# Weight low parts made by accumulating DMAs from GpSimd's queue, and softmax normalization moved from GpSimd to VectorE

## The chip, the cores and the metric

The kernel runs on one core of a Trainium2 chip. The metric is the device time of one execution in microseconds. The kernel before takes 1223.67 us, the median of three runs (1223.36 to 1224.05).

## The reference

One sequence of 512 tokens of width 1024 goes through two transformer blocks, all in float32.

- First block: RMS norm, one wide projection `h @ w_in`, then two attention branches of 8 heads each. One branch keeps the 128 best keys of each query by an indexer score (`relu(q_idx . k_idx)` weighted and summed over 8 index heads); the other is "forgetting" attention, with a cumulative log gate added to its logits. Each branch is gated by a silu and projected; two sigmoid gates from `h @ w_merge` merge the branches; `w_out`, a norm and a gated per-layer embedding (`w_ple`, `w_ple_gate`) follow.
- Second block: RMS norm, a projection `w_in_2`, sliding-window attention with sinks (8 heads), latent attention (8 heads, with `w_uq_2` and `w_ukv_2`), gates `ga` and `gb`, `w_out_2`, then a feed-forward layer `(silu(h @ w_gate_2) * (h @ w_up_2)) @ w_down_2` of inner width 2816, and a final norm.

The weights are float32 and each is read once from HBM. What the document is about is how a weight becomes two matmul operands:

```
w  =  hi + lo          hi = w rounded to the matmul type,  lo = w - hi
x @ w  ~  xh @ hi + xh @ lo + xl @ hi
```

## The kernel before

Every product with a weight runs as three TensorE matmuls (line 345): high by high, activation high by weight low, activation low by weight high. Activations are split into `hh` and `hl` (or `h2h`, `x2h`, `acts`, `fs` and so on) by `split`.

Weights come in one stream of tiles, in an order fixed when the program is built (`stream`, `first_of`). A tile is 128 partitions by at most 1024 columns, 512 KB, mostly two 128-row slices of a 512-column product. For each tile:

- `load_to` issues a DMA on SP's queue into a buffer `raw`, of which there are two;
- `convert_to` rounds it on ScalarE into `wh` (line 260) and subtracts on VectorE to get `wl = raw - wh` (line 261). There are four buffers `wh` and four `wl`. Where `fine[0]` is set, in the interleaved attention stages, both are done in two halves;
- `product` reads both. After the last matmul that reads tile i, `used` calls `convert_to(i + 4)`, which takes the buffers that tile i has left.

The feed-forward's gate and up weights after the first 512 columns go another way (`Quarters`, seven products of quarters, `quart` and `qsum`); they use the same lines 260 and 261. The tile "misc" is made of five column ranges.

`product` has an order. With "mid" it goes through the weight tiles one after the other, four token blocks on each, so that a tile is done with every 24 matmuls. With "all" it goes through all four tiles for the first block, then for the second and so on: the four buffers stay taken until the last block, are released about six matmuls apart, and the next product wants its first tile as soon as this one ends. The name of a product is used in the following for the place where it begins: "the boundary into gb1" is where gb1 follows gb0.

The attention stages are recorded by `interleave`: a step of attention (scores, softmax, and two or three steps later the transposes of the probabilities, then the product with the values) alternates with matmuls of products. There, and in pg1 with q2 and in o21 with fg0 and the quarters, TensorE's order is that of the code (`ordered`). Elsewhere a scheduler orders the instructions of all engines. Each engine and each DMA queue takes its instructions in order.

In `softmax_step`, VectorE adds the mask (line 522), ScalarE exponentiates and sums (line 529), VectorE takes the reciprocal `rr` (line 535), and GpSimd multiplies the probabilities `P` by it (line 537, since `NORM = "pool"`). GpSimd also computes the exponent's bias in the forgetting branch (line 527) and every norm's variance and `rstd` (lines 452 to 463). Before the change it issues no DMA.

Of the kernel before, what the change touches and what calls it, by code (L numbers as in the profile page):

```python
# [13 lines left out]
AF = mybir.ActivationFunctionType  # L14
OP = mybir.AluOpType
# [13 lines left out]
def two_blocks_kernel(  # L29
# [7 lines left out]
    nc = tc.nc  # L37
    pool = ctx.enter_context(tc.tile_pool(name="sb", bufs=1))
# [29 lines left out]
    def blk(i):  # L68
        return slice(i * 128, (i + 1) * 128)

    NORM = "pool"
    TOPK_EVERY = 3
    FOX_EVERY = 3
    IDX = (1.5, 2, 2, 0.5)
# [156 lines left out]
    raws, ws = [], []  # L231
# [3 lines left out]
    def load_to(i):  # L235
        while len(raws) <= min(i, len(stream) - 1):
            pieces, k0, nk, ncols = stream[len(raws)]
            if isinstance(pieces, Quarters):
                raws.append(pieces.load_for(k0))
                continue  # L240
            raw = pool.tile([128, 1024], F32, name="raw", tag="raw", bufs=2)
            raw = raw[:, :nk * ncols].rearrange("p (k c) -> p k c", c=ncols)
            for w, c0, n, at in pieces:
                nc.sync.dma_start(
                    raw[:, :, at:at + n],
                    w[k0 * 128:(k0 + nk) * 128, c0:c0 + n].rearrange("(k p) c -> p k c", p=128))
            raws.append(raw)

    def convert_to(i):
        while len(ws) <= min(i, len(stream) - 1):  # L250
            load_to(len(ws))
            pieces, k0, nk, ncols = stream[len(ws)]
            raw = raws[len(ws)]
            if isinstance(raw, Quarters):
                raw = raw.part(k0)
            hi, lo = [pool.tile([128, 1024], FR, name=t, tag=t, bufs=4)[:, :nk * ncols].rearrange(
                "p (k c) -> p k c", c=ncols) for t in ("wh", "wl")]
            cut = (nk + 1) // 2 if fine[0] else nk
            for js in [slice(j, min(nk, j + cut)) for j in range(0, nk, cut)]:
                nc.scalar.copy(hi[:, js], raw[:, js])  # L260
                mark[0] = nc.vector.tensor_sub(lo[:, js], raw[:, js], hi[:, js].bitcast(F32)).ins  # L261
            ws.append((hi, lo))

    def used(i):
        spent.add(i)
        while upto[0] in spent:
            upto[0] += 1
        convert_to(upto[0] + 3)
        last = min(upto[0] + 5, len(stream) - 1)
        load_to(last - isinstance(stream[last][0], Quarters))  # L270

    side = []
    mark = [None]
# [15 lines left out]
    def product(name, act, evac, tok, order="mid", parts=4, ready=None):  # L289
# [35 lines left out]
        for i, (t, n0, nn, kc) in enumerate(seq):  # L325
            while ready and not ready(kc):
                yield 0
            if t not in ps:
                spare = t == 3 and (ready or order != "all" or ordered_[0] and not fine[0])
                ps[t] = s_bank("mm") if spare else mm_bank()  # L330
            g, j = divmod(kc, step)
            convert_to(f0 + g)
            wh, wl = ws[f0 + g]
            ah, al = act(kc)
# [183 lines left out]
    def softmax_step(Sb, n, mask, sink=None, cq=None):  # L518
# [16 lines left out]
        nc.vector.reciprocal(rr, rs)  # L535
        if NORM == "pool":
            nc.gpsimd.tensor_scalar(P[:, :n], P[:, :n], rr, 1.0, op0=OP.mult, op1=OP.mult)  # L537
# [120 lines left out]
    for tb in range(NB):  # L658
        for c in halves if tb == 0 else [slice(0, 1024)]:
            nc.sync.dma_start(xs[:, tb, c], xv[:, tb, c])  # L660
        if tb == 0:
            gb = g_bcast(g_pre)
        convert_to(tb)
        fine[0] = False
# [144 lines left out]
    def qk_shared(qs, kt, h, Sb, qb, k0, n):  # L809
        nc.tensor.matmul(Sb[:, :n], qs[:, h, blk(qb)], kt[:, 0, k0:k0 + n], start=True, stop=False)  # L810
        nc.tensor.matmul(Sb[:, :n], qs[:, h, blk(qb)], kt[:, 1, k0:k0 + n], start=False, stop=True)  # L811
# [21 lines left out]
    for qb in range(1, NB):  # L833
        n = (qb + 1) * 128
# [59 lines left out]
    for pi in range(4):  # L894
        pair = Pair(lambda att, pi=pi: half_gated(att, aa, pi))
        for h in (2 * pi, 2 * pi + 1):
            steps += causal_head(
                h, lambda Sb, qb, k0, n, h=h: qk_shared(qa, kik[1], h, Sb, qb, k0, n), lambda kb: va[:, kb, :], pair,
# [570 lines left out]
```

## Time and profile before

| What | Value |
|---|---|
| median of three runs | 1223.67 us |
| the profiled execution's own time | 1223.95 us |
| its span, first to last instruction | 1222.2 us |
| TensorE busy | 1188.5 us, 97% of the span |
| VectorE busy | 821.8 us, 67% |
| ScalarE busy | 615.0 us, 50% |
| GpSimd busy | 157.5 us, 13% |
| mean granted TensorE clock | 0.997 |

The shares of the other engines are averages over stages with different loads. TensorE's 97% is the one that matters here: 33.7 us of the span are not matmul. What other engines do costs time only where TensorE has to wait for it. The timeline view has start and duration in microseconds, then the engine, the line, the operation, output and inputs; a release in brackets says how long the engine was idle before and what ended that.

### The profile page before, as it was taken

The numbers are of one execution on the slowest core, as the hardware profiler recorded it, in microseconds if no ns is written. First come the engines' busy times: TensorE is split into PE (matmuls) and PEld (weight loads), VectorE is DVE, ScalarE is ACT, GpSimd is POOL, SyncE is SP. The second block draws the span as 40 slices with busy tenths as digits, with TensorE's granted clock in tenths as the row PEclk, the third lists the DMA queues.
The fourth block names the chain that finished last, engine by engine and source line by source line (L and its number), as shares of the span: only waits on it lengthen the run. The fifth ranks groups of instructions, "written<-read, shape, count | busy, mean of one in ns | idle before, by whom it ended". The sixth has DMA issues, their size and how long they took to land.

```text
span 1222.2 us, 18908 instructions
## 1 busy us (share of the span) xinstructions
PE 1188.5 (97%) x6876; PEld 1030.8 (84%) x6876; DVE 821.8 (67%) x1792; ACT 615.0 (50%) x1290; POOL 157.5 (13%) x307
## 2 busy tenths in 40 slices
PE   6999999999999999999999999999999999999997
PEld 5898888888888888689888889778899999988885
DVE  5578767896676554775555688773887878783322
ACT  4465456545563343534566567632555555472212
POOL 2011033101120022601211112200000000000201
PEclk9999999999999999999999999999999999999999
DMA  5422302321232532324232211353333332253221
GB/s 191 99 68 69 121 19 70 93 87 35 69 105 86 189 121 87 118 86 108 69 89 67 63 62 54 98 172 110 121 104 95 114 107 92 62 173 120 87 86 69
DMA packets 78780, 117.19 MB, mean 96 GB/s; under 512 B 10336, under 2 KB 41312, under 8 KB 78688
## 3 DMA queue, kind: packets, MB, share of 16 engines
q1 hardware_dynamic: 78688, 115.99, 30.1%
q8 instruction: 54, 0.88, 0.3%
q14 instruction: 38, 0.31, 0.1%
HBM read 109.68 MB, written 6.29 MB: 95 GB/s over the span
## 4 chain that ended last, share of the span: by engine, by line
PE 84%; DVE 6%; issue 3%; POOL 2%; ACT 2%; DMA 2%; SPq 0%; POOLq 0%; ACTq 0%; DVEq 0%
PE mm L345 57%; PE mm L1311 7%; PE R L1311 5%; PE E L1311 5%; PE AV L592 3%; PE T L577 3%; DVE wl L261 1%; PE S L810 1%; PE S L811 1%; PE T L476 1%; ACT wh L260 1%; DMA raw<-in_w_in_dram 1%; PE T L1103 1%; DMA quart<-in_w_up_dram 1%; POOL var L461 1%
## 5 line engine op out<-in xcount | busy, mean ns | idle before, releaser
L261 DVE TENSOR_TENSOR wl<-raw,wh 128x512 fp32r<-128x512 f32 (+6 forms) x203 | 186.1, 936 | 139.6 <-ACT wh L260 138.5
L260 ACT CAST wh<-raw 128x512 fp32r<-128x512 f32 (+6 forms) x203 | 158.1, 804 | 192.3 <-PE mm L345 127.8
L345 PE MATMUL mm<-wh,fs 128*128 128x512 f32 x352 | 110.6, 395 | 1.6 <-ACT fs L447 1.6
L537 POOL TENSOR_SCALAR P<-P,rr 128x256 f32<-128x256 f32 (+3 forms) x128 | 68.7, 537 | 310.4 <-DVE rr L535 218.9
L345 PE MATMUL mm<-hh,wh 128*128 128x512 f32 x256 | 103.6, 405 | 0.0
L345 PE MATMUL mm<-hl,wh 128*128 128x512 f32 x256 | 101.4, 396 | 0.0
L345 PE MATMUL mm<-hh,wl 128*128 128x512 f32 x256 | 100.3, 395 | 0.0
L445 DVE TENSOR_TENSOR pl<-T,ph 128x128 fp32r<-128x128 f32 (+3 forms) x152 | 62.3, 412 | 28.7 <-ACT ph L444 28.1
L345 PEld LDWEIGHTS mm<-wh,fs 128*128 128x128 f32 x352 | 65.9, 188 | 18.1 <-ACT fs L447 1.8
L444 ACT CAST ph<-T 128x128 fp32r<-128x128 f32 (+3 forms) x152 | 54.9, 362 | 49.4 <-PE T L577 36.6
L529 ACT ACTIVATE P<-P,nm 128x128 f32<-128x128 f32 (+2 forms) x96 | 51.5, 536 | 47.1 <-DVE nm L522 41.5
L260 ACT CAST wh<-qsum 128x1024 fp32r<-128x1024 f32 (+1 forms) x44 | 42.7, 974 | 54.6 <-PE R L1311 23.2
L345 PE MATMUL mm<-wl,fs 128*128 128x512 f32 x176 | 69.7, 397 | 0.3 <-DVE wl L261 0.3
L261 DVE TENSOR_TENSOR wl<-qsum,wh 128x1024 fp32r<-128x1024 f32 (+1 forms) x44 | 49.5, 1126 | 13.4 <-ACT wh L260 13.4
L1311 PE MATMUL R<-acts,wh 128*128 128x256 f32 x320 | 57.8, 281 | 0.0
L1311 PE MATMUL mm<-acts,wh 128*128 128x256 f32 x320 | 57.6, 280 | 0.0
L345 PEld LDWEIGHTS mm<-hh,wl 128*128 128x128 f32 x256 | 48.0, 188 | 11.2
L1311 PE MATMUL E<-acts,wh 128*128 128x256 f32 x320 | 57.1, 280 | 0.0
L577 PE MATMUL T<-ident,P 128*128 128x128 f32 x296 | 54.5, 277 | 2.4 <-DVE km L445 1.2
L345 PEld LDWEIGHTS mm<-hh,wh 128*128 128x128 f32 x256 | 48.2, 188 | 8.5
L345 PEld LDWEIGHTS mm<-hl,wh 128*128 128x128 f32 x256 | 48.2, 188 | 7.8
L345 PE MATMUL mm<-h2h,wh 128*128 128x512 f32 x128 | 53.4, 417 | 0.0
(392 smaller groups left out, 3344.3 us busy)
## 6 DMA issues: line engine op xcount, KB each, us to landing
raw<-in_w_in_dram SPq DMA_DIRECT2D x50, 512.0 KB, 3.6
raw<-in_w_down_dram SPq DMA_DIRECT2D x22, 512.0 KB, 3.7
quart<-in_w_up_dram SPq DMA_DIRECT2D x20, 512.0 KB, 4.0
raw<-in_w_merge_dram SPq DMA_DIRECT2D x16, 512.0 KB, 3.5
raw<-in_w_out_dram SPq DMA_DIRECT2D x16, 512.0 KB, 3.7
quart<-in_w_gate_dram SPq DMA_DIRECT2D x16, 512.0 KB, 3.7
raw<-in_w_ple_gate_dram SPq DMA_DIRECT2D x8, 512.0 KB, 3.8
raw<-in_w_branch_b_dram SPq DMA_DIRECT2D x4, 512.0 KB, 3.5
```

What stands on the lines that cost most here:

```text
L260: nc.scalar.copy(hi[:, js], raw[:, js])
L261: mark[0] = nc.vector.tensor_sub(lo[:, js], raw[:, js], hi[:, js].bitcast(F32)).ins
L345: nc.tensor.matmul(o, x_, m, start=kc == 0 and k == 0 and n0 == 0, stop=last and k == 2)
L444: nc.scalar.copy(hi, src)
L445: nc.vector.tensor_sub(lo, src, hi.bitcast(F32))
L461: nc.gpsimd.tensor_scalar(v, ss[:, 1:2], 1.0 / n, v, op0=OP.mult, op1=OP.add)
L476: nc.tensor.transpose(T[:, i, :], src[:, blk(c + i)], ident)
L529: nc.scalar.activation(P[:, :n], P[:, :n], AF.Exp, bias=bias, scale=-1.0, accum_out=rs)
L537: nc.gpsimd.tensor_scalar(P[:, :n], P[:, :n], rr, 1.0, op0=OP.mult, op1=OP.mult)
L577: nc.tensor.transpose(T[:, i, :], P[:, blk(i)], ident)
L592: nc.tensor.matmul(self.av[:, q0:q0 + pc.stop - pc.start], self.v(kb), m, start=pi == 0 and i == 0, stop=pi == len(plan) - 1 and i == 1)
L1311: nc.tensor.matmul(R[:, c, :], w[:, kc, cs], m[:, kc, :], start=first and c + kc + k == 0, stop=kc == 3 and k == 2, skip_group_check=True)
```

## The change

For a weight tile of one column range (not "misc", not the quarters, and not the first four tiles of the program), the low part is no longer subtracted on VectorE. ScalarE writes the rounded tile negated into `wl`; then a DMA issued from GpSimd's queue reads the weight a second time from HBM and adds it to what stands in `wl`. The two halves of the `fine` stages fall away for these tiles: there is one instruction of each kind per tile. And the probabilities are multiplied by the reciprocal on VectorE.

```
-    NORM = "pool"
+    NORM = "dve"
...
             hi, lo = [pool.tile([128, 1024], FR, name=t, tag=t, bufs=4)[:, :nk * ncols].rearrange(
                 "p (k c) -> p k c", c=ncols) for t in ("wh", "wl")]
+            if len(ws) > 3 and not isinstance(pieces, Quarters) and len(pieces) == 1:
+                w, c0, n, _ = pieces[0]
+                nc.scalar.copy(hi, raw)
+                mark[0] = nc.scalar.activation(lo, raw, AF.Copy, scale=-1.0).ins
+                nc.gpsimd.dma_start(lo, w[k0 * 128:(k0 + nk) * 128, c0:c0 + n].rearrange("(k p) c -> p k c", p=128),
+                                    accum_op=OP.add)
+                ws.append((hi, lo))
+                continue
             cut = (nk + 1) // 2 if fine[0] else nk
```

Lines after the added ones are eight higher in the changed kernel: line 345 is 353 there, 537 to 539 are 545 to 547.

ScalarE's queue at the boundary into gb1, before (`wh` and `raw` are the weight tile, `tb` a gate's output, `ph` the high part of transposed probabilities, `P` the probabilities, `es` the sink's term):

```order
L444 CAST ph<-T 128x128
L260 CAST wh<-raw 128x512 x2
L444 CAST ph<-T 128x128
L260 CAST wh<-raw 128x512 x2
L529 ACTIVATE P,rs<-P,nm 128x256
L532 ACTIVATE es<-sk,nm 128x1
L444 CAST ph<-T 128x128 x2
L529 ACTIVATE P,rs<-P,nm 128x256
L532 ACTIVATE es<-sk,nm 128x1
L864 ACTIVATE tb_5905<-mm 128x512
L260 CAST wh<-raw 128x512 x4
L529 ACTIVATE P,rs<-P,nm 128x128
```

ScalarE's queue at the same place, with the change:

```order
L872 ACTIVATE tb_5940<-mm 128x512
L452 CAST ph<-T 128x128
L260 CAST wh<-raw 128x1024
L261 ACTIVATE wl<-raw 128x1024
L452 CAST ph<-T 128x128
L260 CAST wh<-raw 128x1024
L537 ACTIVATE P,rs<-P,nm 128x256
L540 ACTIVATE es<-sk,nm 128x1
L261 ACTIVATE wl<-raw 128x1024
L452 CAST ph<-T 128x128
L260 CAST wh<-raw 128x1024
L261 ACTIVATE wl<-raw 128x1024
```

What VectorE did in halves now stands on ScalarE behind the rounding, as one instruction, in front of the exponentials and splits of the attention steps.

GpSimd's queue in the forgetting attention, before (`bias` is the exponent's bias, `P` the probabilities):

```order
L527 TENSOR_SCALAR bias<-nm,ctok 128x1
L537 TENSOR_SCALAR P<-P,rr 128x128
L527 TENSOR_SCALAR bias<-nm,ctok 128x1
L537 TENSOR_SCALAR P<-P,rr 128x256
L527 TENSOR_SCALAR bias<-nm,ctok 128x1
L537 TENSOR_SCALAR P<-P,rr 128x384
```

GpSimd's queue there with the change (`in_w_merge_dram` are the weights of ma0 and ma1, which run inside this stage):

```order
L262 DMA wl<-in_w_merge_dram 128x2x512 x3
L535 TENSOR_SCALAR bias<-nm,ctok 128x1
L262 DMA wl<-in_w_merge_dram 128x2x512
L535 TENSOR_SCALAR bias<-nm,ctok 128x1 x13
L262 DMA wl<-in_w_merge_dram 128x2x512
L535 TENSOR_SCALAR bias<-nm,ctok 128x1
L262 DMA wl<-in_w_merge_dram 128x2x512 x2
```

The multiplications have left GpSimd, and the weights' DMAs stand between the biases. Each DMA waits at the head of this queue until ScalarE has written its tile.

VectorE's queue in the same stage with the change (`S` are the scores, `pl` the low part of the transposed probabilities):

```order
L543 RECIPROCAL rr<-rs 128x1
L530 ISA P,nm<-S,causal 128x256
L530 ISA nm 128x1
L547 TENSOR_SCALAR P<-P,rr 128x128
L543 RECIPROCAL rr<-rs 128x1
L530 ISA P,nm<-S,causal 128x384
```

The multiplication is queued one mask step behind its reciprocal.

## Rows read from the trace of the kernel before

**Rows 1.** The page: busy time of each engine, share of span, instructions.

```profile
PE 1188.5 (97%) x6876; PEld 1030.8 (84%) x6876; DVE 821.8 (67%) x1792; ACT 615.0 (50%) x1290; POOL 157.5 (13%) x307
```

**Rows 2.** What TensorE waited for: us in total, times, longest.

```profile
PE T L476 <- DVE xn L670: 9.6, 1, 9.6
PE T L476 <- DVE xn L484: 4.0, 3, 2.2
PE mm L345 <- DVE wl L261: 3.0, 3, 2.2
...
PE T L577 <- POOL P L537: 0.2, 1, 0.2
```

**Rows 3.** Groups by form: busy us, mean ns, then idle time before.

```profile
L261 DVE TENSOR_TENSOR wl<-raw,wh 128x1024 fp32r<-128x1024 f32 x88 | 110.5, 1259 | 116.8 <-ACT wh L260 116.5
L260 ACT CAST wh<-raw 128x1024 fp32r<-128x1024 f32 x88 | 92.3, 1049 | 150.3 <-PE mm L345 112.5 <-issue 19.4 <-DMA raw<-in_w_in_dram 5.4
L537 POOL TENSOR_SCALAR P<-P,rr 128x256 f32<-128x256 f32 x48 | 25.1, 524 | 104.7 <-DVE rr L535 54.2 <-ACT ph L444 12.9 <-ACT ta L864 10.6
L527 POOL TENSOR_SCALAR bias<-nm,ctok 128x1 f32<-128x1 f32 x32 | 11.7, 365 | 43.9 <-DVE nm L522 43.5
```

**Rows 4.** Timeline at the boundary into gb1: its third weight tile.

```profile
658.92 1.77 SPq L244 DMA_DIRECT2D raw<-in_w_in_dram  x2
...
662.69 1.13 ACT L260 CAST wh<-raw 128x512 fp32r<-128x512 f32 x2
...
664.28 0.69 DVE L261 TENSOR_TENSOR wl<-raw,wh 128x512 fp32r<-128x512 f32 x1
...
665.02 0.39 PE L345 MATMUL mm<-h2h,wl 128*128 128x512 f32 x1
```

**Rows 5.** Timeline, tight boundaries: subtraction and first reader, into vb and dn0.

```profile
100.41 1.71 DVE L261 TENSOR_TENSOR wl<-raw,wh 128x512 fp32r<-128x512 f32 x2
...
102.05 0.39 PE L345 MATMUL mm<-wl,hh 128*128 128x512 f32 x1
...
1087.35 1.22 DVE L261 TENSOR_TENSOR wl<-raw,wh 128x1024 fp32r<-128x1024 f32 x1
...
1088.62 0.74 PE L345 MATMUL mm<-wl,fs 128*128 128x512 f32 x2 [0.33 <-DVE wl L261]
```

**Rows 6.** Timeline, middle boundaries: the same pair, into mb0 and o21.

```profile
280.56 1.22 DVE L261 TENSOR_TENSOR wl<-raw,wh 128x1024 fp32r<-128x1024 f32 x1
...
283.94 0.39 PE L345 MATMUL mm<-hh,wl 128*128 128x512 f32 x1
...
837.87 1.23 DVE L261 TENSOR_TENSOR wl<-raw,wh 128x1024 fp32r<-128x1024 f32 x1 [0.43 <-ACT wh L260]
...
840.98 0.39 PE L345 MATMUL mm<-wl,yh 128*128 128x512 f32 x1
```

**Rows 7.** Timeline, wide boundaries: the same pair, into qb and ga0.

```profile
36.43 1.23 DVE L261 TENSOR_TENSOR wl<-raw,wh 128x1024 fp32r<-128x1024 f32 x1 [0.72 <-ACT wh L260]
...
41.19 0.40 PE L345 MATMUL mm<-hh,wl 128*128 128x512 f32 x1
...
581.14 1.22 DVE L261 TENSOR_TENSOR wl<-raw,wh 128x1024 fp32r<-128x1024 f32 x1
...
586.44 0.40 PE L345 MATMUL mm<-h2h,wl 128*128 128x512 f32 x1
```

**Rows 8.** DMA issues: count, size of each, median us from issue to landing.

```profile
raw<-in_w_in_dram SPq DMA_DIRECT2D x50, 512.0 KB, 3.6
...
x4d<-x SPq DMA_DIRECT2D x4, 512.0 KB, 2.6
...
xs<-in_x_dram SPq DMA_DIRECT2D x3, 512.0 KB, 10.3
```

**Rows 9.** Windows: busy us (and count) of PE, PEld, DVE, ACT, POOL; clock, DMA.

```profile
870.00:900.00 30.00, 27.78 (x222) 27.45 (x221) 24.93 (x32) 15.82 (x24) 0.00 (x0) 0.94 0.28 87
```

**Rows 10.** Timeline: a multiplication by a scalar on VectorE.

```profile
284.18 0.41 DVE L842 TENSOR_SCALAR mk<-mk 128x512 f32<-128x512 f32 x1
```

## Prediction

> **What bounds the kernel now.** I read the page's busy times first. The reader is to see that TensorE is busy for 1188.5 us of 1222.2, so that 33.7 us at most can be won anywhere, and every new wait of TensorE is paid in full [rows 1]. Then what TensorE waited for: 9.6 and 4.0 us are the first norm, before any weight matters to this change; the subtraction that makes `wl` cost 3.0 us in three waits; GpSimd's multiplication of the probabilities 0.2 us [rows 2]. So neither of the two things that the change takes off VectorE and GpSimd holds TensorE up. What remains is the timeline at the places where one product's weights follow another's: how long before its first reader was each `wl` ready? This gap is the room that the change may use up.
>
> **The change, part by part.** Durations are of the profiled execution, 1223.95 us (span 1222.2), 0.3 us over the median of the runs; the sum is made on 1224.
>
> *The new path of a low part.* Before, ScalarE rounds a 1024-column tile in 1.05 us and VectorE subtracts in 1.26 us, or in two halves [rows 3]. Now ScalarE makes a second copy of 1.05 us, which ends about 0.2 us before the subtraction did (at the boundary into gb1 the rounding of the third tile starts at 662.69, so the copy would end at 664.79, and the subtraction ended at 664.97 [rows 4]). Behind it comes a DMA that has no counterpart in the trace: GpSimd issues it when the copy is done, it fetches 512 KB from HBM, and adds them to 512 KB in SBUF. Call X the time from GpSimd's issue until the sum has landed. A low part is then ready d = X - 0.2 later than before.
>
> X is bounded by rows of transfers of the same size. It can't be under 3.6 us, the plain load of the same bytes, since it does that load and more. The longest is 10.3 us, loads in the crowd at the start. I take the value that follows from what has to be moved: the load's 3.6 plus reading the old contents out of SBUF, for which the store of 512 KB stands with 2.6, makes 6.2 [rows 8]. So d is 6.0, with ends 3.4 and 10.1. All 145 affected tiles pay d; it costs time only where the gap is shorter. In the middle of a product of order "mid" the tile is converted three tiles ahead, and d is hidden by the matmuls of the two tiles before it. At boundaries it isn't, because four buffers are all there are: a tile can't be started before the old product has left its buffer.
>
> *The gaps.* Of each boundary I take the tile with the shortest gap from the end of the subtraction to the first matmul that reads the tile (stalls of one boundary don't add up, since the later tiles are wanted later by as much). There are 25 with a gap below 6 us, in three groups:
> - Eight tight ones, 0 to 0.5 us, mean 0.15: into vb, pg1, q2, gb0, gb1, os1, fg0 and dn0. The first ends at 102.12 and is read at 102.05 (the second half is wanted a little later), the last ends at 1088.57 and is read at 1088.62 [rows 5].
> - Eight middle ones, 1.1 to 2.2 us, mean 1.55: into mb0, mb1, kv2, ga1, os0, os2, os3 and o21; the first from 281.78 to 283.94, the last from 839.10 to 840.98 [rows 6].
> - Eight wide ones, 2.9 to 4.5 us, mean 3.65: into qb, kb, gate_b, ma0, qa, yb0, ql and ga0; the first from 37.66 to 41.19, the last from 582.36 to 586.44 [rows 7]. And ma1 with 5.6.
>
> With d = 6.0 TensorE waits 8 x 5.85 = 46.8, 8 x 4.45 = 35.6, 8 x 2.35 = 18.8 and 0.4 us: 102 us. With 3.4 it is 26.0 + 14.8 + 1 = 42; with 10.1 it is 79.6 + 68.4 + 51.6 + 4.5 = 204.
>
> The Trainium skill's page "DMA: Bandwidth & Descriptors", section "Anatomy of one DMA", fits DMAs of GpSimd's queue as 2.0 us plus bytes over 436 GB/s. For a plain copy of 512 KB that makes an estimate of 3.2 us; no run here shows one, and the loads of SP's queue take 3.6 [rows 8]. By it the waits would be 35 us.
>
> *What is queued behind the waiting DMA.* GpSimd's queue is in order, and each DMA stands there until ScalarE has written its tile, which itself waits for TensorE to leave the buffer. Behind it are the biases of the forgetting branch, 32 of 0.37 us [rows 3], and the `rstd` of the norms. The bias leads to an exponential whose result is transposed two steps later. I price this at nothing; without that cover it would be one wait of a few us at each of the two boundaries inside that stage, 0 to 8 us.
>
> *ScalarE.* It gets 145 x 1.05 = 152 us more, 767 of 1222. An exponential behind a copy starts 1.05 us later; the two or three steps until its transposes hide that. I take 0. Without cover it would be 1.05 for each of the 32 tiles that are converted in the sliding-window and latent attention, 34 us.
>
> *VectorE and GpSimd.* VectorE loses 145 x 1.26 = 183 us [rows 3] and gets 128 multiplications. None like them is in the trace, but one by a constant of the largest size takes 0.41 us there [rows 10], so at most 52 us; GpSimd takes 0.52 for the middle size [rows 3]. With 0.2 us of waiting for that result now [rows 2], the move itself is worth nothing. VectorE becomes free earlier, which can give back some of TensorE's idle time: 33.7 less the first norm's 13.6 and the 3.0 that are replaced leave 17 as the bound. Much of that is the end of the program. I take 6.
>
> The Trainium skill's page "SBUF — State Buffer", section "SBUF: two separate sides", says that GpSimd can't write the descriptors of its DMAs while VectorE runs an instruction that takes both ports, and such a multiplication is one. Rows can't show it, as there is no such DMA yet. It would add to X at most the 0.41 of one multiplication, in the attention stages alone: some 17 boundaries, 7 us.
>
> *The clock.* Around the boundary into fg0, where TensorE waits for late weights, the granted clock over 870 to 900 is 0.94 [rows 9]: 6% of 30 us at the lower of its two levels, 1.2 GHz, costs 1.8 us. Longer waits at the eight tight boundaries may bring the same, 0 to 14 us. I take 4.
>
> Sum: 1224 + 102 - 6 + 4 = 1324 us.
>
> **The rivals.**
> 1. *The addition costs no more than a plain load*, X about 3.6: for it speaks that the same 16 engines do both, and they were busy for a share of 0.28 in the window of [rows 9]. Then 42 us of waits: 1224 + 42 - 6 = 1260 us. It decides when the landing, as the trace gives it, lies under 4.5 us.
> 2. *The addition is much slower*, X of 8.5 and more, because reading, adding and writing back don't overlap, or because the raw loads of the next tiles run at the same time on the same engines. At 10.3: 1224 + 204 - 6 + 10 of the clock = 1432 us; at 8.5, some 160 of waits, 1380.
> 3. *The landing is hidden and VectorE's relief decides*: faster. The place is the eight tight boundaries; with the scheduler ordering other matmuls into the gaps, or an X under 1.7 us (8 x 1.35 = 11 us of waits at the most), the 6 to 17 us that VectorE gives back outweigh them: 1212 us. Against it: in the attention stages, in pg1 with q2 and in fg0, TensorE's order is that of the code, and X under the plain load's 3.6 has no row.
>
> **How the numbers follow.** Forecast (X between 4.5 and 8.5) 0.52, rival 1 0.22, rival 2 0.19, rival 3 0.07. The time is the likeliest's, 1324 us. For 8 in 10 the range goes down to 1258, just below rival 1, and up to 1425, short of rival 2 at its longest; the uncertain covers (ScalarE 34, biases 8, clock 14) lie inside it. A difference below 0.2% can't be told from none here. Only rival 3 is not slower: faster 0.05, same 0.02, slower 0.93.
>
> **What the profile after would show.** Right: TensorE's waits name a landing DMA or `wl` at the boundaries listed, about 4 to 6 us each at the tight ones, and next to nothing inside dn0 and out0; the issue list shows 145 DMAs on GpSimd's queue at about 6 us; VectorE is some 130 us less busy, ScalarE some 150 more; the quarters between fg0 and dn0 take as long as before. Wrong: if the landing is at 6 us and TensorE doesn't wait, the gaps were not what holds; if TensorE waits as much for exponentials, splits or transposes as for weights, ScalarE was mis-priced; if waits inside "mid" products appear, X is far above the range taken.

## The result, and the profile after

The changed kernel takes 1418.08 us (median of 4 runs, 1416.59 to 1422.04), the kernel before 1223.86 us on the same chip (4 runs, 1223.36 to 1229.3). The ratio is 1.158, with a 95% interval of 1.154 to 1.1621. The forecast was 1324 us: the direction was right, and 1418 lies inside the range of 1258 to 1425, but 194 us were lost where 100 were forecast.

First the page's busy times, in the form of [rows 1], and the DMA queues (packets, MB, share of the 16 engines' time):

```profile
span 1415.8 us, 18702 instructions
...
PE 1248.6 (88%) x6876; PEld 1064.5 (75%) x6876; DVE 699.3 (49%) x1724; ACT 739.3 (52%) x1384; POOL 254.9 (18%) x324
...
q0 software_dynamic: 41744, 73.15, 30.0%
q1 hardware_dynamic: 78688, 115.99, 27.1%
```

VectorE is 122.5 us less busy and ScalarE 124.3 more, so the work moved as the diff says. TensorE runs the same 6876 matmuls but is busy for 60.1 us more: it ran slower. The span grew by 193.6 us, so the other 133.5 us are idle time of TensorE (span less busy time: 33.7 before, 167.2 now).

Then what TensorE waited for, in the form of [rows 2]:

```profile
PE mm L353 <- DMA wl<-in_w_in_dram: 50.8, 22, 5.4
PE mm L353 <- DMA wl<-in_w_merge_dram: 19.1, 11, 3.6
PE mm L353 <- DMA wl<-in_w_o_swa_dram: 18.5, 3, 7.6
PE mm L353 <- DMA wl<-in_w_gate_dram: 13.1, 4, 6.8
PE T L484 <- DVE xn L678: 9.5, 1, 9.5
PE mm L353 <- DMA wl<-in_w_out_dram: 7.9, 4, 4.6
PE mm L353 <- DMA wl<-in_w_ple_gate_dram: 7.5, 4, 2.3
PE mm L353 <- DMA wl<-in_w_branch_b_dram: 5.0, 1, 5.0
PE mm L353 <- DMA wl<-in_w_branch_a_dram: 3.9, 1, 3.9
```

The accumulating DMAs that write `wl` have taken the place of VectorE's 3.0 us. I put each wait down to the tile whose landing ended it. They sum to 129 us: 54 at the eight tight boundaries, 39 at the middle ones, 23 at the wide ones, 5 at ma1 and 8 elsewhere (into uq0 and ya1 and inside out1, which the prediction doesn't list). They replace VectorE's 3.0 us, so 126 us are new; all other idle time together went from 30.7 to 38.3 us.

Why do the low parts come so late? The DMA issues (count, size, median us from issue to landing), in the form of [rows 8]:

```profile
raw<-in_w_in_dram SPq DMA_DIRECT2D x50, 512.0 KB, 5.8
wl<-in_w_in_dram POOLq DMA_DIRECT2D x46, 512.0 KB, 8.2
raw<-in_w_down_dram SPq DMA_DIRECT2D x22, 512.0 KB, 7.8
wl<-in_w_down_dram POOLq DMA_DIRECT2D x22, 512.0 KB, 8.7
...
raw<-in_w_out_dram SPq DMA_DIRECT2D x16, 512.0 KB, 7.7
wl<-in_w_out_dram POOLq DMA_DIRECT2D x16, 512.0 KB, 9.5
```

X was taken as 6.2 us; it is 8.2 in the median of the 145. The raw loads of the same weights went from 3.6 to 5.8 us. By the queue rows a packet of the accumulating DMAs takes a DMA engine 0.300 x 16 x 1415.8 / 41744 = 163 ns in the mean, one of SP's queue 78. These two don't compare like with like, since SP's queue has many smaller packets: of those of 2048 bytes, the trace gives an accumulating one 186 ns and one of SP's queue 110.

The timeline at the boundary into gb1 shows what becomes of it. TensorE's four waits for the product's four tiles come first, then GpSimd's four issues (start, us; idle time before, with what ended it, in brackets):

```profile
785.28 0.80 PE L353 MATMUL mm<-h2h,wl 128*128 128x512 f32 x1 [4.70 <-DMA wl<-in_w_in_dram]
789.90 0.50 PE L353 MATMUL mm<-h2h,wl 128*128 128x512 f32 x1 [1.50 <-DMA wl<-in_w_in_dram]
793.17 0.50 PE L353 MATMUL mm<-h2h,wl 128*128 128x512 f32 x1 [1.38 <-DMA wl<-in_w_in_dram]
796.56 0.50 PE L353 MATMUL mm<-h2h,wl 128*128 128x512 f32 x1 [0.60 <-DMA wl<-in_w_in_dram]
...
777.37 1.21 POOL L262 DMA_DIRECT2D wl<-in_w_in_dram  x1 [24.38 <-ACT ph L452]
780.10 1.20 POOL L262 DMA_DIRECT2D wl<-in_w_in_dram  x1 [1.52 <-ACT ph L452]
783.22 1.20 POOL L262 DMA_DIRECT2D wl<-in_w_in_dram  x1 [1.91 <-ACT wl L261]
790.35 1.20 POOL L262 DMA_DIRECT2D wl<-in_w_in_dram  x1 [5.93 <-ACT wl L261]
```

In [rows 4] the third tile was read 0.05 us after its subtraction. Now the first matmul on a low part starts at 785.28, 7.9 us after the first issue, and the four waits make 8.2 us. The fourth issue is late for another reason: ScalarE had to wait for the tile's raw load, and rounds and negates only behind it.

```profile
788.05 1.04 ACT L260 CAST wh<-raw 128x1024 fp32r<-128x1024 f32 x1 [3.83 <-DMA raw<-in_w_in_dram]
```

Over the run such waits of ScalarE went from 41.8 to 61.0 us; how much of TensorE's waits comes from them was not tried alone.

Last the clock, in windows (us of the stretch; busy us of PE, PEld, DVE, ACT, POOL; granted clock; DMA share; GB/s), in the form of [rows 9]:

```profile
740.00:760.00 20.00, 13.03 (x49) 9.98 (x48) 4.79 (x20) 9.30 (x23) 3.63 (x3) 0.74 0.93 207
770.00:800.00 30.00, 21.82 (x104) 16.84 (x103) 10.31 (x40) 17.26 (x41) 4.82 (x4) 0.94 0.60 125
1030.00:1065.00 35.00, 21.93 (x129) 19.66 (x128) 15.50 (x22) 18.50 (x29) 6.87 (x8) 0.85 0.69 165
1080.00:1230.00 150.00, 150.00 (x1271) 150.00 (x1270) 125.95 (x129) 77.67 (x98) 0.00 (x0) 1.00 0.35 104
1320.00:1350.00 30.00, 30.00 (x130) 24.11 (x129) 2.75 (x4) 13.05 (x19) 11.65 (x11) 1.00 0.93 188
```

At the boundaries into gb0, gb1 and fg0 (the first three rows) TensorE idles for 7 to 13 us and is granted its lower level, 1.2 GHz, for part of the stretch. Inside the quarters and inside dn0 and dn1 (the last two) it neither waits nor slows, the latter although the DMA engines are 0.93 busy. Over the run the trace has 2 stretches at the lower level before, 10.6 us in all, and 26 after, 145 us in all, 3.41 to 10.24 us each; all but the last, at the program's end, begin in or behind waits of TensorE.

### The profile page after: what moved, and what is told of

It reads as the page before. It is cut to its first block, busy times and chain, and to the rows that moved or that the text cites. A ratio compares the mean times of both kernels' runs of the same rounds, so it can differ in the third digit from the quotient of the medians.

```text
span 1415.8 us, 18702 instructions
## 1 busy us (share of the span) xinstructions
PE 1248.6 (88%) x6876; PEld 1064.5 (75%) x6876; DVE 699.3 (49%) x1724; ACT 739.3 (52%) x1384; POOL 254.9 (18%) x324
## 3 DMA queue, kind: packets, MB, share of 16 engines
q0 software_dynamic: 41744, 73.15, 30.0%
## 5 line engine op out<-in xcount | busy, mean ns | idle before, releaser
L261 ACT ACTIVATE wl<-raw 128x1024 fp32r<-128x1024 f32 (+3 forms) x145 | 148.4, 1024 | 106.8 <-PE mm L353 85.9
L260 ACT CAST wh<-raw 128x1024 fp32r<-128x1024 f32 (+3 forms) x145 | 146.2, 1008 | 88.8 <-PE mm L353 35.1
L353 PE MATMUL mm<-hh,wl 128*128 128x512 f32 x256 | 104.5, 417 | 28.8 <-DMA wl<-in_w_merge_dram 19.1
L262 POOL DMA_DIRECT2D wl<-in_w_in_dram x53 | 64.6, 1218 | 251.5 <-ACT wl L261 220.6
L353 PE MATMUL mm<-hh,wh 128*128 128x512 f32 x256 | 106.7, 418 | 0.0
L353 PE MATMUL mm<-hl,wh 128*128 128x512 f32 x256 | 104.6, 409 | 0.0
L262 POOL DMA_DIRECT2D wl<-in_w_down_dram x22 | 26.4, 1200 | 299.8 <-ACT wl L261 299.8
L353 PE MATMUL mm<-h2h,wl 128*128 128x512 f32 x128 | 53.9, 421 | 23.8 <-DMA wl<-in_w_in_dram 23.8
```

The lines of the kernel that those rows point to most:

```text
L260: nc.scalar.copy(hi, raw)
L261: mark[0] = nc.scalar.activation(lo, raw, AF.Copy, scale=-1.0).ins
L262: nc.gpsimd.dma_start(lo, w[k0 * 128:(k0 + nk) * 128, c0:c0 + n].rearrange("(k p) c -> p k c", p=128), accum_op=OP.add)
L353: nc.tensor.matmul(o, x_, m, start=kc == 0 and k == 0 and n0 == 0, stop=last and k == 2)
```

## The experiments

Theory: a low part lands some 8 us late, which is paid where the gap at a boundary is shorter, and paid again in TensorE's clock. The rivals: the division on VectorE, ScalarE's second copy, GpSimd's issue, DMA traffic as such, or a cost per DMA wherever it stands. In the table, "idle" is span less busy time of TensorE, "half" the time at its lower clock level of 1.2 GHz (the half clock), and X the median from issue to landing of GpSimd's DMAs; all but the ratios are in us.

| run | us | ratio to before | PE busy | idle | half | X |
|---|---|---|---|---|---|---|
| before | 1223.9 | | 1188.5 | 33.7 | 10.6 | |
| after | 1418.1 | 1.154 to 1.162 | 1248.6 | 167.2 | 145 | 8.2 |
| 1 division only | 1229.0 | 1.003 to 1.006 | 1190.9 | 36.7 | 14 | |
| 2 addition on VectorE | 1254.8 | 1.023 to 1.029 | 1202.8 | 56.2 | 25 | |
| 3 DMA without addition | 1303.6 | 1.062 to 1.067 | 1215.3 | 86.3 | 62 | 4.9 |
| 4 DMA only | 1428.3 | 1.163 to 1.170 | 1257.9 | 173.9 | 167 | 8.5 |
| 5 no raw loads | 1319.6 | 1.073 to 1.080 | 1224.9 | 95.5 | 79 | 6.0 |
| 6 inner tiles only | 1230.7 | 1.004 to 1.007 | 1193.7 | 34.9 | 21 | 8.9 |
| 7 tight tiles only | 1300.6 | 1.060 to 1.064 | 1216.1 | 83.7 | 80 | 8.5 |
| 8 filled waits | 1410.8 | 1.149 to 1.157 | 1315.3 | 96.2 | 59 | 8.2 |
| 9 fitted filling | 1407.4 | 1.148 to 1.153 | 1285.9 | 118.7 | 76 | 8.4 |
| 10 low parts last, after | 1438.0 | 1.173 to 1.182 | 1260.1 | 172.1 | 183 | 8.7 |
| 11 low parts last, before | 1268.3 | 1.033 to 1.038 | 1204.0 | 60.7 | 30 | |

### 1 and 4: the two halves of the change

```diff
@@ 1: before
-    NORM = "pool"
+    NORM = "dve"
@@ 4: after
-    NORM = "dve"
+    NORM = "pool"
```

> The kernel before with only the probabilities' division moved to VectorE. Theory (the loss comes from the low parts that land late): this half of the change is worth nothing, 1224 us, at most 3 us either way, VectorE busy about 5 us more. Rival (the division delays VectorE's other work in the attention and with it the conversions): over 1230 us, up to what separates this from 1418.

> The kernel after with the probabilities' division back on GpSimd. Theory: as the kernel after, 1418 us, within 5 us. Rival (the division on GpSimd stands in the way of the accumulating DMAs' issue, or its absence on VectorE frees the conversions): differs from 1418 by more than 10 us, upwards to 1430 for the first, downwards to 1400 for the second.

Measured: 1229.04 and 1428.26 us. The DMAs make the loss, and the division isn't part of it. It isn't quite nothing, though: alone it costs 5 us (ratio 1.0025 to 1.0055), and beside the DMAs having it on GpSimd costs 10, more than the 5 that I allowed. The 10 us are the number that the rival of run 4 named, but its mechanism isn't seen: in both traces GpSimd issues a DMA 0.30 us (median) behind ScalarE's second copy, 2.1 us at the most. With the division on GpSimd the low parts land a little later (8.5 for 8.2 us) and the half clock is 22 us longer; why was not tried.

### 2: the second copy without the DMA

```diff
-                nc.gpsimd.dma_start(lo, ..., accum_op=OP.add)
+                mark[0] = nc.vector.tensor_add(lo, raw, lo.bitcast(F32)).ins
```

> The kernel after, with ScalarE's copy and negated copy of whole tiles kept, but the addition made by VectorE from the raw tile instead of by a DMA. Theory (the DMA's 8 us from issue to landing is what costs): the low part now comes after 1.05 + 1.06 + 1.25 = 3.4 us of conversion in place of 1.3 for a first half, 2.1 us later than before; at the 8 tight boundaries that is 8 x (2.1 - 0.15) = 16, at the middle ones 8 x (2.1 - 1.55) = 4, so 1240 us, 1230 to 1255. Rival (ScalarE's 124 us of additional work, or whole tiles in place of halves, is what costs): 1330 us or more, near the 1418 of the kernel after.

Measured: 1254.79 us, at the upper end of the theory's range and 163 under the kernel after. ScalarE does as much here (739.6 us) as there. What TensorE waits for most:

```profile
PE mm L352 <- DVE wl L262: 10.4, 11, 2.0
```

For the softmax's tiles it waits some 8 us that it didn't wait for before. So the second copy, whole tiles and the addition on VectorE are worth at most 1255 - 1229 = 26 us, and don't make the loss.

### 3 and 5: what the landing consists of

```diff
@@ 3: after, the DMA overwrites
-                                    accum_op=OP.add)
@@ 5: after, zeros in place of the raw loads of the affected tiles
+            if len(raws) > 3 and len(pieces) == 1:
+                raws.append(zero[:, None, :ncols].to_broadcast([128, nk, ncols]))
+                continue
```

> The kernel after, where GpSimd's DMA copies the weights over the low part and doesn't add (the low part is then the whole weight: the addition is left out). Same issues, same bytes read, same queue. Theory (the addition takes about twice the DMA engines' time per packet, 163 ns against 78, and company of raw loads stretches it): start to landing falls from 8.1 to about 5 us, the tight boundaries wait 8 x 4.7 = 38, the middle 8 x 3.3 = 26, the wide 8 x 1.2 = 10, with the half clock behind the waits some 30 more: 1310 us, 1285 to 1340. Rival (the delay is GpSimd's issue and its queue, not the addition): 1400 to 1420, landing still about 8 us. Rival (plain-rate landing of 3.6 us): 1260.

> The kernel after without the raw loads of the tiles whose low part comes by the accumulating DMA: ScalarE copies and negates a constant zero tile instead, and the DMA adds the weights onto it (the high part is then zero: that part of the product is left out). The 145 accumulating DMAs stay. Theory (6.1 us alone, 8.2 in the company of raw loads): start to landing falls to about 6.2, so the tight boundaries wait 8 x 5.9 = 47, the middle 8 x 4.4 = 35, the wide 8 x 2.3 = 18, in all 100 in place of some 160, and the half clock behind the waits costs 45 in place of 70: 1360 us, 1330 to 1385. Rival (an accumulating DMA takes 8 us whatever runs beside it): landing stays at 7.5 or more, time over 1395. Rival (the kernel after is bound by the DMA engines as a whole, twice the bytes): 1280 or less.

Measured: 1303.60 us without the addition, as expected, and 1319.59 us without the raw loads, where 1360 (1330 to 1385) was expected: the landing is what I said, but it costs less. Queues and issues of the run without the addition:

```profile
q1 hardware_dynamic: 78688, 115.99, 26.8%
q0 software_dynamic: 41744, 73.15, 19.6%
...
wl<-in_w_in_dram POOLq DMA_DIRECT2D x46, 512.0 KB, 4.9
...
wl<-in_w_down_dram POOLq DMA_DIRECT2D x22, 512.0 KB, 4.3
```

and of the run without the raw loads:

```profile
q0 software_dynamic: 41744, 73.15, 33.8%
q1 hardware_dynamic: 36944, 42.84, 10.0%
wl<-in_w_in_dram POOLq DMA_DIRECT2D x46, 512.0 KB, 6.0
wl<-in_w_down_dram POOLq DMA_DIRECT2D x22, 512.0 KB, 5.9
```

Per packet the DMA engines need 98 ns for the copy (0.196 x 16 x 1301.6 / 41744) and 163 to 171 ns with the addition, in company or not; these are the same packets, so they compare. Among packets of 2048 bytes it is 111 ns for the copy and 186 to 196 with the addition, and 96 for one of SP's queue beside the copies: the addition is dear, not GpSimd's queue. Run 3's expectation set 163 against the 78 of SP's queue, and so made the addition dearer, next to a load, than it is. The landing takes 4.9 us for a copy beside raw loads, 6.0 for an addition without them, 8.2 for an addition beside them. Both the addition and the company are needed for 8.2. GpSimd's own part in it is small. Its instruction takes 0.5 us less without the addition, of the 3.3 us that the landing is shorter, and in run 5 it takes 1.2 us as before, though the landing is 2.2 us shorter:

```profile
L262 POOL DMA_DIRECT2D wl<-in_w_in_dram x53 | 64.6, 1218 | 251.5 <-ACT wl L261 220.6 <-ACT ph L452 30.9
...
L262 POOL DMA_DIRECT2D wl<-in_w_in_dram x53 | 38.9, 735 | 231.1 <-ACT wl L261 199.8 <-ACT ph L451 31.3
```

(busy us, mean ns, idle before; the first is the kernel after, the second run 3).

### 6 and 7: the same DMA at places with and without a gap

```diff
@@ 6: with the division on GpSimd
+    inner = {first_of[n] + i for n in ("out0", "out1", "pg0", "o20") for i in range(4)}
+    inner |= {first_of[n] + i for n in ("dn0", "dn1") for i in range(11)} - {first_of["dn0"], first_of["dn0"] + 1}
...
-            if len(ws) > 3 and ... and len(pieces) == 1:
+            if len(ws) > 3 and ... and len(pieces) == 1 and len(ws) in inner:
@@ 7: the same with
+    tight = {first_of[n] + i for n in ("vb", "pg1", "q2", "gb0", "gb1", "fg0") for i in range(4)}
+    tight |= {first_of["os1"], first_of["dn0"], first_of["dn0"] + 1}
```

> The division on GpSimd as in the kernel before, and the accumulating DMA only for the 36 tiles of four products and of the last one that follow a gap of 9 us or more: out0, out1, pg0, o20 and the tiles of dn0 and dn1 but the first two. Theory (a late low part costs only what the gap doesn't cover): 1224 us, 1219 to 1230, though a quarter of the DMAs run. Rival (each DMA costs about the same wherever it stands, 194 / 145 = 1.3 us, by DMA traffic, ScalarE's work or GpSimd's): 1224 + 48 = 1272, 1255 to 1290.

> The kernel after with the accumulating DMA only for the 27 tiles of the eight tight boundaries (vb, pg1, q2, gb0, gb1, fg0 with four tiles each, the first tile of os1, the first two of dn0). Theory: 8 waits of 8.2 - 0.15 less what fewer loads in company take off, 8 x 7.5 = 60, half clock behind them 25, the division on VectorE 5: 1314 us, 1290 to 1330. Rival (the loss is spread evenly over the DMAs): 1224 + 27 x 1.3 + 5 = 1264, under 1275.

Measured: 1230.69 us with 36 DMAs in the gaps (7 us, 0.2 us for each DMA) and 1300.55 us with 27 at the tight boundaries (77 us, 5 of them the division's: 2.6 us for each). What TensorE waits for in the run with the inner tiles:

```profile
PE mm L355 <- ACT junk L478: 2.0, 1, 2.0
...
PE mm L355 <- DMA wl<-in_w_ple_gate_dram: 0.4, 1, 0.4
```

and in the run with the tight ones:

```profile
PE mm L355 <- DMA wl<-in_w_in_dram: 24.1, 9, 4.6
PE mm L355 <- DMA wl<-in_w_gate_dram: 11.7, 4, 6.9
...
PE mm L355 <- DMA wl<-in_w_ple_gate_dram: 7.8, 4, 2.5
PE mm L355 <- DMA wl<-in_w_o_swa_dram: 6.3, 1, 6.3
```

The DMAs land as late in both (8.9 and 8.5 us). In the gaps that costs 0.4 us of waiting; at the tight boundaries 50 us, with 28 us more of TensorE's busy time. A fixed cost of 1.3 us per DMA is ruled out by both. The 7 us of the inner tiles are just above the range: they come with 10.6 us more at half clock, 6.8 of them in two stretches behind waits of 2.0 us (the row for `junk`, a square on ScalarE) and 2.3 us that the kernel before doesn't have there, and 3.4 in one at the boundary into dn0, behind a wait of 1.6 us that the kernel before has as well, without such a stretch.

### 8 and 9: filling the waits

```diff
+            for _ in range(FILL.get(name, 0) if i == 0 else 0):
+                nc.tensor.matmul(o, *ops[0], start=True, stop=True)
             for k, (x_, m) in enumerate(ops):
```

> The kernel after with matmuls of no use ahead of the first one of 24 products (26 each at the tight boundaries, 20 at the middle, 10 at the wide; they repeat the first product of the high part into the bank that is started afresh behind them, so the output is the same): some 90 us of TensorE's time, meant to lie inside the waits. Theory (TensorE's half clock comes behind the idle waits and costs some 60 to 70 of the 194 us): the half-clock time falls from 145 us to under 80, and the kernel takes 1375 us, 1345 to 1400, though it does more work. Rival (the waits alone make the loss, the clock next to nothing): 1415 us or more.

> As the run with the matmuls of no use, but their number fitted to the wait that the trace of the kernel after shows at each product's first tile (vb 7, q2 22, os3 30, ...), 16 products, some 66 us in all, so that they lie inside the waits. Theory (the half clock comes behind the waits and costs 0.46 us per us of it; the earlier run didn't get faster because 36 of its 107 us of such matmuls ran past the waits): TensorE's idle time falls by about 60 us, the half clock from 145 to some 80 us, 30 us come back, 1388 us, 1370 to 1403. Rival (what the clock gives back is lost again, since the next low part comes when its DMA lands and not when TensorE is done): 1408 us or more, whatever the clock.

Measured: 1410.84 and 1407.38 us, outside the ranges of the theory and near what the rivals give (1415 and 1408 or more). Only the second is better than the kernel after clear of noise, and barely: the interval of its ratio ends at 1.153, that of the kernel after begins at 1.154, and the first run's goes up to 1.157. The matmuls of no use, in the trace of the first (stretch; PE busy; clock; DMA share; GB/s):

```profile
0.00:1411.00 1411.00, 107.06 (x448) 0.98 0.57 135
```

and of the second:

```profile
0.00:1404.00 1404.00, 63.09 (x286) 0.97 0.58 136
```

The half clock falls from 145 to 59 and 76 us, and the kernel's own matmuls get faster: 1315.3 - 107.1 = 1208.2 and 1285.9 - 63.1 = 1222.8 us, against 1248.6. So the waits do cause the half clock, at 0.37 to 0.47 us per us of it. But in the second run the 26 us that came back shortened the span by 11 only. The waits at the first tiles went, and those at the next tiles grew (into q2 the second tile's from 1.6 to 3.1 us, into gb1 from 1.5 to 2.6): the waits for low parts fell from 129 to 81 us, not by the 63 filled. A faster TensorE reaches the next late low part earlier.

### 10 and 11: using the low parts last

```diff
+    HI, LO = (0, 1), (2,)
...
+            seq = [q + (ks,) for r in runs_ for ks in (HI, LO) for q in r]
...
-            for k, (x_, m) in enumerate(ops):
-                nc.tensor.matmul(o, x_, m, start=kc == 0 and k == 0 and n0 == 0, stop=last and k == 2)
+            for k in ks:
+                nc.tensor.matmul(o, *ops[k], start=kc == 0 and k == 0 and n0 == 0, stop=last and k == 2)
```

> The kernel after with the products' order changed: of a block (two row chunks for four token blocks, or all chunks for one token block) the 16 matmuls on high parts come first, then the 8 on low parts; before, each low part was used 0.24 to 0.5 us behind its high part. Theory (the loss is the time from high part to low part that nothing covers): 16 x 0.24 = 3.9 us of cover at each of the 24 boundaries, where 117 of the 130 us of waits lie; the waits fall to about 65, the half clock from 145 to 75 us, so 130 - 65 = 65 and 32 less: 1321 us, 1290 to 1360. Rival (DMA traffic sets the pace): over 1395.

> The same order of high and low products put into the kernel before, whose low parts come from VectorE 0.2 us behind the high ones. Theory: TensorE waits there for low parts 3 us in all, so at most that goes: 1222 us, 1217 to 1230. Rival (the buffers of both parts are held longer when the low products come last, and the conversions come late): 1235 or more.

Measured: 1437.96 and 1268.25 us, both slower than without the new order; the theory's numbers fell. TensorE's waits in the first:

```profile
PE mm L365 <- DMA wl<-in_w_in_dram: 46.2, 19, 7.2
PE mm L365 <- ACT wh L260: 35.4, 15, 5.3
```

and in the second:

```profile
PE mm L357 <- ACT wh L260: 12.5, 14, 2.3
```

The waits for low parts fell to 93 us, not to 65, and new ones for high parts came. By its number run 10 fits its rival of DMA traffic as well (over 1395), but run 11 has the new order without these DMAs and loses 45 us by it, so run 10 can't decide between the two. Run 11 fits its own rival: where the low parts come last, four pairs of buffers come free later, and so the next tiles' conversions start later. That the buffers are the reason wasn't tried alone.

## Why the prediction was right, and where it fell short

*What bounds the kernel.* Right. TensorE was 97% busy, each new wait was paid, and nothing that VectorE was relieved of came back.

*X.* The step "the load's 3.6 plus reading the old contents out of SBUF, 2.6, makes 6.2" comes near the number of an accumulating DMA without raw loads beside it: 6.0 us (run 5). That it is made of these two parts no run shows. In the kernel it runs beside the raw loads, and it is 8.2. The cause stood in rival 2 ("because the raw loads of the next tiles run at the same time on the same engines"), while its other cause alone, an addition that doesn't overlap, would have left 8.5 or more in run 5. The bound of 10.3 held in the median of every target (10.0 at most), not for each DMA: a tenth of them took 10.4 us or more.

*The gaps.* Right in place: 116 of 129 us of waits are at the 24 listed boundaries, and none in out0 and inside dn0. The size: 102 forecast, 129 measured. The rule by the shortest gap gives too much once X is known: with d = 8.0 it makes 63 + 52 + 35 + 2 = 152. It does so in the runs 3 and 5 as well (69 for 45 measured, 96 for 59), so the two errors went against each other. "Stalls of one boundary don't add up" holds for gb1, whose four waits make 8.2 us, but not for fg0, where they make 13.1; into vb and dn0 there is less than one whole wait (2.7 and 0.5 us). Why those gaps were wider than the subtraction's end and the first read say stays open.

*The clock.* This is the step that failed: "I take 4", with 14 as the bound. TensorE's busy time grew by 60.1 us. The row that I read it from, 0.94 over 870 to 900, had one wait and one stretch of 3.41 us (11% of the window at the lower level, not 6%; the cost of 1.8 us is right, since half of the clock is lost there). I multiplied it by eight boundaries, where the waits came at 24, several to a boundary, and brought 26 stretches of up to 10.24 us. The filled waits show that these are the waits' doing. They also show that the 60 us are not a loss on top that could be had back whole: of 26 us that the clock gave back in run 9, 15 went into later waits and into filling that overran.

*VectorE's relief and ScalarE.* -6 and 0 were forecast; idle time outside the low parts is up by 7.6 us. TensorE now waits 2.0, 1.9 and 1.7 us for ScalarE at three kinds of place where it didn't. The bound of the relief was misread too: the 4.0 us of waits for `xn` that the prediction puts to the first norm lie between 503 and 522 us, at the second block's first norm, so that 21 us and not 17 were left. The longest of them, before:

```profile
521.87 1.07 PE L476 MATMUL T<-ident,xn 128*128 128x128 f32 x8 [2.17 <-DVE xn L484]
```

With the change these waits are gone, but they are gone in run 7 too, where VectorE keeps nearly all of its work; there as here TensorE waits for late low parts of pg1 and q2 around that norm. No run shows a gain from VectorE's relief itself.

*The division.* "Worth nothing" was off by 5 us (run 1). The Trainium skill's page "SBUF — State Buffer", section "SBUF: two separate sides", would have GpSimd's descriptors wait for VectorE's two-port instructions. No run shows it: with the division on VectorE the low parts land at 8.2 us, with it on GpSimd at 8.5.

The sum, in span: 102 - 6 + 4 = 100 was forecast, 125.9 + 7.6 + 60.1 = 193.6 measured, with the 3.0 us that were replaced taken off the 128.9. Of the 93.6 us that were missing, 24 are waits for low parts, 13.6 the relief and ScalarE, and 56 the clock. That 1418 still fell inside the range, 7 us below its upper end, is in part luck: the range left 14 us for the clock, which took 60, and what made up for it was room for longer waits, which the rule of the gaps had put too high.

## What to carry to other kernels

A transfer put into the path from a buffer's release to its first reader costs what the schedule's gap there doesn't cover of its landing, and next to nothing where the gap is wide: the same accumulating DMA cost 2.6 us at a tight boundary and 0.2 us in a wide gap. Size it by transfers in the company that it will have, since the load beside it made 8.2 us of 6.0. Where TensorE is to wait in many places, read a row of its clock behind one such wait, and multiply by all the waits, not by the large ones; hiding one wait may only move it to the next tile.

## What the runs showed of the hardware

- A packet of 2048 bytes took a DMA engine 186 to 196 ns where it was added to SBUF, 111 where GpSimd's queue copied it into the same tiles, and 96 to 110 on SP's queue (kernel after, runs 3 and 5). Beside additions the raw loads of `in_w_in` landed in 5.8 us in place of 3.6, beside GpSimd's copies in 4.4.
- GpSimd is busy 1.2 us for each accumulating DMA and 0.7 for a copy (the rows of the kernel after and of run 3 above). The 145 make some 175 us; its busy time rose by 97, since the division left it, which took 65.5 off by itself (157.5 to 92.0 in run 1). It held little up: 0.30 us from the end of ScalarE's copy to the issue in the median, 2.1 at the most.
- A copy of 512 KB by GpSimd's queue, beside raw loads, landed in 4.9 us in the median and 3.9 at the least (run 3; 4.2 to 6.2 in the medians by target). The Trainium skill's page "DMA: Bandwidth & Descriptors", section "Anatomy of one DMA", makes an estimate of 3.2 us of it; the measurement decides.
- The half clock came with short waits too: behind 2.0 and 2.3 us in run 6, with 3.41 us at 1.2 GHz each. With these two and a third such stretch TensorE's busy time rose by 5.2 us.
